# Who reads the second mixer's transposes, and how many copies of the relative bias lie in DRAM

## Chip, cores and metric

The kernel runs on one core of one Trainium2 chip. The metric is the device time of one execution in microseconds (us), the median of several runs. The inputs come from DRAM, the output goes back there.

## What is computed

Two blocks of two layers each on 256 tokens of width 1024. In the first block a layer is a mixer (grouped attention and dilated attention) and a mixture of 16 experts; the second block's layers are a gated linear attention and a differential attention, each followed by a mixture of 16 experts. Two pieces matter here. The first is the start of a layer of the first block: the layer's input is normalised, scaled and shifted by the condition, and multiplied by `w_in`:

```python
for l in range(DEPTH):                       # DEPTH = 2
    mod = cond @ w_ada[l] + b_ada[l]
    sh1, sc1, g1, sh2, sc2, g2 = [m[:, None, :] for m in jnp.split(mod, 6, axis=-1)]
    h = _layer_norm(x) * (1.0 + sc1) + sh1
    mix = _mixer(h, w_in[l], ...)
    x = _layer_norm(DN_ALPHA * x + g1 * mix, ln1_g[l], ln1_b[l])
    h = _layer_norm(x) * (1.0 + sc2) + sh2
    ffn = _moe(h, w_router, router_bias, w_exp_gate[l], w_exp_up[l], w_exp_down[l])
    x = _layer_norm(DN_ALPHA * x + g2 * ffn, ln2_g[l], ln2_b[l])
```

The second is the relative bias of the differential attention, which depends only on the distance of two tokens and the head:

```python
bias = rel_table[rel_bucket(kpos[None, :] - qpos[:, None])].transpose(2, 0, 1)
s = jnp.einsum('bhqd,bhkd->bhqk', qb, kk).astype(jnp.float32) * scale + bias
```

## The kernel before

The 256 tokens are two row tiles of 128. A product with 32-bit weights is made of three: weights and activations are split into a part that is rounded to the matrix engine's format and the rest, `whi` and `wlo`, `hh` and `hl`, and `acc` sums whi·hh, whi·hl and wlo·hh (L427). ScalarE writes `whi` (L346), VectorE and, at the borders between stages, GpSimd write `wlo` (L356). The stages follow each other on the same `x`: mixer 0, moe10, mixer 1, moe11, then the second block with moe20 and moe21; while one stage runs, SyncE loads the weights of those that follow.

**The border.** `block1(l, prev)` is a mixer of the first block. For its second call `prev` is the end of moe10. For each row tile VectorE writes `z` in two halves (L1251), TensorE turns it in two groups of four 128x128 pieces into a PSUM tile `pt` (`transposed`, L321), and `ev` brings each piece to SBUF, scaled by `sc1` and shifted by `sh1`, which are values per partition once `z` is turned. `ev` writes the result twice: ScalarE as `hh` (L1240, rounded by the write), VectorE as `hf` (L1241, unrounded); then VectorE subtracts for `hl` (L1243). `hf` has two buffers. Between the row tiles VectorE finishes `x` of row tile 1 (L297, L302) and GpSimd helps with `wlo`. The products of the first two weight columns start while the second row tile is still underway.

**The relative bias.** `bias_task` runs as a side task of mixer 1. It makes one row of 384 values for each of 8 heads (`fsb`, 8 partitions) and a DMA on ScalarE's queue writes it into DRAM as `fd` (L1542). In the second block `diff` reads it back (L1783), on ScalarE's queue too, so that partition p gets 256 values that begin at 127 − p: row p of the table is the same row shifted by one. The read steps 383 values from partition to partition, so each partition reads a copy of its own. The reads go into buffers that the weights of moe20 leave, while its last `y` products run.

**Order.** Which instruction follows which on an engine is settled when the program is built, by the recorded order of the code and by planners that place side tasks. Loads of weights are issued by SyncE in program order (L193); each waits for its buffer. There are eight semaphores for hardware DMAs, DMAHW0 to DMAHW7, given out in turn over all DMAs of the program, whichever engine issues them; a DMA waits until the one that had its semaphore before, eight DMAs back, has landed.

Of the kernel before, what the change touches and what calls it, by code (L numbers as in the profile page):

```python
# [10 lines left out]
F32 = mybir.dt.float32  # L11
# [3 lines left out]
AF = mybir.ActivationFunctionType  # L15
OP = mybir.AluOpType
# [3 lines left out]
P = 128  # L20
# [96 lines left out]
SM_TICKS = 4  # L117
JOB_GAP = 2
P_BUFS = 4
S_BANKS = 3  # L120
DEC = 4
TAGS = ("moe10", "moe11", "moe20", "moe21")
# [8 lines left out]
def body(ctx: ExitStack, tc: tile.TileContext, A: dict, out: bass.AP, dbg=None):  # L131
    nc = tc.nc
    PE, V, S, G = nc.tensor, nc.vector, nc.scalar, nc.gpsimd
# [9 lines left out]
    dram = ctx.enter_context(tc.tile_pool(name="dr", bufs=1, space=DRAM))  # L143
# [858 lines left out]
    def residual(fl, gp, xh, xl, late, lanes, rows, hold, route, logits, gate=None):  # L1002
# [38 lines left out]
        def scores(tt, k0, m):  # L1041
            if k0 == 0:
                rp[tt] = ps.tile([P, 512], F32, tag="s2", name="rp", bufs=S_BANKS)
            for k in range(k0, k0 + m):
# [117 lines left out]
    def block1(l, prev):  # L1162

        with tc.tile_pool(name="gp", bufs=1, reuse_waits="tile") as gp:
            gates[l, 1] = gp.tile([P, D], F32, name="g2")
            es = gp.tile([P, 2, NE], F32, name="es")
            with ExitStack() as stack:
# [7 lines left out]
                hh = gp.tile([P, KC, T], F32R, tag="hh", name="hh")  # L1175
# [17 lines left out]
                sh1, sc1 = modc[l][:, 0:8], modc[l][:, 8:16]  # L1193
# [41 lines left out]
                def ev(tt, q, pt):  # L1235
                    ts = slice(tt * P, (tt + 1) * P)
                    t = dl.tile([P, 4, P], F32, tag="hf", name="hf", bufs=2)
                    for c in range(4):
                        k = 4 * q + c
                        S.activation(hh[:, k, ts], pt[:, c], AF.Identity, bias=sh1[:, k:k + 1], scale=sc1[:, k:k + 1])  # L1240
                        V.tensor_scalar(t[:, c], pt[:, c], sc1[:, k:k + 1], sh1[:, k:k + 1], op0=OP.mult, op1=OP.add)  # L1241
                    dst = (slice(None), slice(4 * q, 4 * q + 4), ts)
                    V.tensor_tensor(hl[dst], t, hh[dst].bitcast(F32), op=OP.subtract)  # L1243

                if prev is not None:
                    for tt in range(2):
                        if tt == 1:
                            for _ in prev.affine(1):
                                pass
                        for hs in (slice(0, 512), slice(512, 1024)):  # L1250
                            V.tensor_scalar(z[:, tt, hs], X[:, tt, hs], *prev.mr[tt], op0=OP.subtract, op1=OP.mult)  # L1251
                        if tt == 0:
                            prev.second()
                        prev.lows()
                        transposed(ps, "tp", z[:, tt], tt, ev)
                    chain_ends()
# [83 lines left out]
                def global_job(tt, c):  # L1340

                    s2 = [ps.tile([P, 2, 256], F32, tag="s2", name="s2", bufs=S_BANKS) for _ in range(2)]
                    for j in range(2):
# [5 lines left out]
                    for v in range(2):  # L1349
# [3 lines left out]
                        V.scalar_tensor_tensor(nm, nm, -1.0, sc, op0=OP.mult, op1=OP.mult)  # L1353
                        p = d2.tile([P, 2, 256], F32, tag="p", name="p", bufs=P_BUFS)
                        sums = sm.tile([P, 2], F32, tag="sums", name="sums")
# [30 lines left out]
                def dil_job(tt, c):  # L1386
                    pr = []
                    s2 = [ps.tile([P, 512], F32, tag="s2", name="s2d", bufs=S_BANKS) for _ in range(2)]
                    rows_ = [slice(64 * hf, 64 * hf + 64) for hf in range(2)]
# [10 lines left out]
                    for hf in range(2):  # L1400
                        slope = 2.0 ** (-8.0 * (2 * c + hf + 1) / 12)
                        p = d2.tile([P, 384], F32, tag="p", name="pd", bufs=P_BUFS)
                        V.tensor_scalar(p[:, 0:256], nb[:, tt * T:(tt + 1) * T], slope, None, op0=OP.mult)
# [43 lines left out]
                if l + 1 == DEPTH:  # L1447
                    fl.add("ada", bias_task(ps, d2))
# [42 lines left out]
                for u in range(4):  # L1491
                    wh, wl = fl.get()
                    fl.ahead()
                    for m in range(2):
# [4 lines left out]
                        t = dl.tile([P, 2, T], F32, tag="hf", name="mt", bufs=2)  # L1499
# [16 lines left out]


    lam = cst.tile([P, 4], F32, name="lam")
    fd = dram.tile([8, P, 384], F32, name="fd")
    fap = fd[:]  # L1520

    def bias_task(ps, pool):


        oh1 = pool.tile([32, 512], F32, tag="pT", name="ohb", bufs=3)
        S.dma_start(oh1, A["bucket"])
        rt = pool.tile([32, 8], F32, tag="adas", name="rt8")
        S.dma_start(rt, A["rel_table_2"])
        ab = []
        for nm in "qk":  # L1530
            t = pool.tile([P, 128], F32, tag="adab", name="lq")
            for i in range(2):
                src = A[f"b_lam_{nm}{i + 1}_2"][0]
                S.dma_start(t[:, 64 * i:64 * i + 64], bass.AP(tensor=src.tensor, offset=src.offset, ap=[[0, P], [1, 64]]))
            ab.append(t)
        yield LAM_WAIT
        pf = ps.tile([P, 512], F32, tag="tp", name="pf")
        PE.matmul(pf[0:8, :], rt, oh1, start=True, stop=True)
        yield 1
        fsb = pool.tile([8, 384], F32, tag="pT", name="fsb", bufs=3)  # L1540
        V.tensor_copy(fsb, pf[0:8, :384])
        S.dma_start(fd, fsb[:, None, :].to_broadcast([8, P, 384]))  # L1542
        yield 2
        t = pool.tile([P, 128], F32, tag="adas", name="ltm")
        tc.keep_in_program_order(V.tensor_tensor(t, ab[0], ab[1], op=OP.mult))
        V.tensor_reduce(lam[:, 0:2], t.rearrange("p (i e) -> p i e", i=2), axis=AX.X, op=OP.add)
        yield 1
        S.activation(lam[:, 0:2], lam[:, 0:2], AF.Exp)
        V.tensor_tensor(lam[:, 2:3], lam[:, 0:1], lam[:, 1:2], op=OP.subtract)
        V.tensor_scalar(lam[:, 3:4], lam[:, 2:3], LAMBDA_INIT, -1.0, op0=OP.add, op1=OP.mult)  # L1550
# [189 lines left out]
    def diff(prev, gp, room, load_router, logits, rows):  # L1740
        with tc.tile_pool(name="dl", bufs=1, reuse_waits="tile") as dl, tc.tile_pool(name="d", bufs=1, reuse_waits="tile") as d, tc.tile_pool(name="d2", bufs=2, reuse_waits="tile") as d2, \
# [3 lines left out]
            def slot(i, shape, name):  # L1745
                return room[i].tile([P] + shape, F32, tag="w", name=name)

            hh = gp.tile([P, KC, T], F32R, tag="hh", name="hh4")
# [31 lines left out]
            v = [t[:, 0].rearrange("p (t n) -> p t n", t=2) for t in vb]  # L1780
            Tb = [t[:, 1].rearrange("p (h n) -> p h n", h=4) for t in vb]
            for i in range(2):
                S.dma_start(Tb[i], bass.AP(tensor=fap.tensor, offset=fap.offset + 127 + i * 4 * P * 384,  # L1783
                                           ap=[[383, P], [P * 384, 4], [1, 256]]))
            pbuf = slot(7, [4, 2, 256], "pbuf")
            pairs = [(0, 1), (2, 3)]
            gs = row_bcast(d, "gs", A["b_g_sub_2"][0])
# [7 lines left out]
            def job(tt, hp):  # L1795
                nk = (tt + 1) * P
                ws = []
                pair = pairs.pop(0)
                s2 = [ps.tile([P, 512], F32, tag="s2", name="s2f", bufs=S_BANKS) for _ in range(2)]
                for i in range(2):  # L1800
# [80 lines left out]
    def block2(l, prev):  # L1881
        with ExitStack() as es:
            gp = es.enter_context(tc.tile_pool(name="gp", bufs=1, reuse_waits="tile"))
            room = [es.enter_context(tc.tile_pool(name=f"ring{i + 3}", bufs=1, reuse_waits="tile")) for i in range(8)]
            lg, el = gp.tile([P, 2, 4], F32, name="lg"), gp.tile([P, 2, NE], F32, name="el")

            cols = gp.tile([P, 2, KC], F32, name="cols")
            shifts = []

            def load_router():  # L1890
                S.dma_start(cols, A["ln_cols"][:, l])
                route = router(gp, [A["moe_w_group_2"][l], A["moe_w_router_2"][l]],
                               [A["moe_b_group_2"][l], A["moe_b_router_2"][l].rearrange("g j -> (g j)")])
                shifts.append(route[2][:, 1])
                return route, cols

            def logits(tt, t, sd):
                b = shifts[0]
                V.scalar_tensor_tensor(lg[:, tt], t[:, 0:4], sd, b[:, 0:4], op0=OP.mult, op1=OP.add)
                V.scalar_tensor_tensor(el[:, tt], t[:, 4:20], sd, b[:, 4:20], op0=OP.mult, op1=OP.add)  # L1900

            z = (gla if l == 0 else diff)(prev, gp, room, load_router, logits, lambda: rows_of(A["ln_g_2"][l, 0], A["ln_b_2"][l, 0]))
            return moe(z, 2, SLOTS2[l], (lg, el), A["moe_w_gate_2"][l], A["moe_w_up_2"][l], A["moe_w_down_2"][l], None, None,
                       f"moe2{l}", lambda: rows_of(A["ln_g_2"][l, 1], A["ln_b_2"][l, 1], True), False, room=room)
# [49 lines left out]
```

## Time and profile before

| | before |
|---|---|
| median of 3 runs (lowest to highest) | 1602.59 us (1598.65 to 1603.44) |
| profiled execution, and its span | 1602.16 us, 1600.4 us |
| TensorE (PE) busy | 1470.0 us, 92% of the span |
| VectorE (DVE), ScalarE (ACT), GpSimd (POOL) busy | 869.0, 432.8, 129.2 us |
| DMA, mean | 288 GB/s |
| mean granted clock of TensorE | 0.969 of full speed |

Times of rows are in us from the start of the span. A granted clock of 1.00 is the upper of TensorE's two levels (2.4 GHz), 0.50 the lower (1.2 GHz). In a timeline each row gives the start, the time until the end of the last of the instructions put together in it, the engine, the line, the operation and its tiles, their count, and in brackets how long the engine had stood idle before and what released it. Engines with a q are their instruction queues, where a DMA issue counts with the time that the issue itself stood. In a row of waits stand the engine, the line and tile that waited, what it waited for, then the sum, the number of waits and the longest.

### The profile page before, as it was taken

To read this page: it belongs to the slowest core of one execution; us is meant where nothing else is said; L and a number is where in the kernel's file an instruction comes from. 1 tells how busy PE (TensorE), PEld (TensorE's weight loads), DVE (VectorE), ACT (ScalarE), POOL (GpSimd) and SP (SyncE) were. 2 spreads that over 40 slices of the span, in tenths; PEclk is the share of its full clock that TensorE was granted. 3 is DMA by queue.
4 is the path that set the end of the run, shared out by engine and by line. 5 is a ranking of instruction groups with operands and counts; after the bars stand their busy time and mean duration, and the time that the engine had idled before them with its cause. 6 is when DMAs were issued, how large, how long until landed. Compare 5 with 4: busy or idle time off the path is not lost. (4 is left out here: it accounts for less than half of the span.)

```text
span 1600.4 us, 22811 instructions
## 1 busy us (share of the span) xinstructions
PE 1470.0 (92%) x9124; PEld 969.4 (61%) x9124; DVE 869.0 (54%) x1686; ACT 432.8 (27%) x733; POOL 129.2 (8%) x140
## 2 busy tenths in 40 slices
PE   4999987998889999889989999999998999999895
PEld 3879987443478999734448895443337988434331
DVE  3689998343678879823464574231127776212214
ACT  1454331211235434111125331110103652101000
POOL 0200002000121000300011001000003002000001
PEclk9999999999979999889999999999999999999998
DMA  9978799995855769799887487999999966999993
GB/s 301 365 249 273 259 303 324 353 302 198 268 174 173 242 232 337 167 363 359 292 263 214 133 290 267 386 387 353 381 334 288 298 195 244 341 386 387 346 386 124
DMA packets 324371, 461.69 MB, mean 288 GB/s; under 512 B 20077, under 2 KB 178285, under 8 KB 324258
## 3 DMA queue, kind: packets, MB, share of 16 engines
q1 hardware_dynamic: 308720, 446.34, 81.5%
q10 hardware_dynamic: 15538, 13.81, 3.5%
q8 instruction: 76, 1.25, 0.3%
q14 instruction: 37, 0.30, 0.1%
HBM read 456.43 MB, written 3.67 MB: 287 GB/s over the span
## 5 line engine op out<-in xcount | busy, mean ns | idle before, releaser
L786 PE MATMUL gu<-w,xg 128*64 128x512 f32 x1536 | 369.2, 597 | 0.0
L786 PEld LDWEIGHTS gu<-w,xg 128*64 128x64 f32 x1536 | 110.8, 137 | 209.1 <-issue 202.7
L356 DVE TENSOR_TENSOR wlo<-w,whi 128x2048 fp32r<-128x2048 f32 (+2 forms) x92 | 183.3, 1994 | 44.9 <-ACT whi L346 44.2
L850 PE MATMUL y<-w,sa 128*64 128x512 f32 x768 | 195.6, 607 | 4.4 <-DMA w<-in_w_exp_down_dram 4.4
L346 ACT ACTIVATE whi<-w 128x2048 fp32r<-128x2048 f32 (+2 forms) x92 | 157.9, 1726 | 151.4 <-PE acc L427 111.6
L850 PEld LDWEIGHTS y<-w,sa 128*64 128x64 f32 x768 | 55.0, 138 | 106.0 <-issue 97.7
L830 DVE SCALAR_TENSOR_TENSOR sa<-gu,cr,sa 128x256 f32<-128x256 f32 (+1 forms) x32 | 19.7, 615 | 163.6 <-PE gu L786 136.4
L334 PE MATMUL sc<-yy,st 128*128 128x512 f32 x256 | 88.8, 436 | 18.1 <-ACT yy L860 14.3
L522 DVE SCALAR_TENSOR_TENSOR adac<-w,ce,adac 128x512 f32<-128x512 f32 x140 | 104.7, 748 | 1.2
L427 PE MATMUL acc<-hl,whi 128*128 128x256 f32 x608 | 93.3, 286 | 0.0
L427 PE MATMUL acc<-hh,whi 128*128 128x256 f32 x608 | 90.4, 289 | 1.6 <-ACT whi L346 1.6
L892 DVE TENSOR_TENSOR x<-x,sc 128x512 f32<-128x512 f32 x112 | 74.3, 683 | 30.4 <-PE sc L334 30.3
L427 PE MATMUL acc<-hh,wlo 128*128 128x256 f32 x608 | 85.9, 281 | 0.0
L334 PE MATMUL pg<-oh,zh 128*128 128x256 f32 x256 | 73.8, 319 | 13.1 <-DVEq L907 7.3
L334 PEld LDWEIGHTS sc<-yy,st 128*128 128x128 f32 x256 | 42.0, 188 | 70.7 <-ACT yy L860 36.0
L427 PEld LDWEIGHTS acc<-hh,whi 128*128 128x128 f32 x608 | 78.4, 190 | 6.8 <-issue 4.1
L427 PE MATMUL acc<-whi,hh 128*128 128x256 f32 x416 | 70.9, 303 | 12.2 <-ACT hh L1240 8.9
L427 PEld LDWEIGHTS acc<-hl,whi 128*128 128x128 f32 x608 | 79.6, 189 | 3.7 <-issue 3.2
L427 PEld LDWEIGHTS acc<-hh,wlo 128*128 128x128 f32 x608 | 77.3, 188 | 1.0 <-issue 0.8
L334 PEld LDWEIGHTS pg<-oh,zh 128*128 128x128 f32 x256 | 55.4, 218 | 27.8 <-issue 15.0
L334 PE MATMUL pg<-oh,zl 128*128 128x256 f32 x256 | 71.2, 308 | 0.9 <-issue 0.9
L860 ACT ACTIVATE yy<-y 128x512 fp32r<-128x512 f32 x32 | 19.1, 597 | 192.2 <-PE y L850 192.2
(376 smaller groups left out, 2107.8 us busy)
## 6 DMA issues: line engine op xcount, KB each, us to landing
w<-in_moe_w_gate_dram SPq DMA_DIRECT2D x64, 1024.0 KB, 12.1
w<-in_moe_w_up_dram SPq DMA_DIRECT2D x64, 1024.0 KB, 13.8
w<-in_moe_w_down_dram SPq DMA_DIRECT2D x128, 512.0 KB, 11.6
w<-in_w_ada_dram SPq DMA_DIRECT2D x47, 1024.0 KB, 7.2
w<-in_w_in_dram SPq DMA_DIRECT2D x40, 1024.0 KB, 5.6
w<-in_w_exp_gate_dram SPq DMA_DIRECT2D x64, 512.0 KB, 9.5
w<-in_w_exp_up_dram SPq DMA_DIRECT2D x64, 512.0 KB, 8.8
w<-in_w_exp_down_dram SPq DMA_DIRECT2D x64, 512.0 KB, 8.9
```

The costliest lines, as they stand in the source:

```text
L334: PE.matmul(dst, l, r, start=(i == 0), stop=(i == n - 1), skip_group_check=True)
L346: S.activation(hi[:, k0:k0 + n], w, AF.Copy)
L356: eng.tensor_tensor(lo[:, k0 + x:k0 + y], w[:, x:y], hi[:, k0 + x:k0 + y].bitcast(F32), op=OP.subtract)
L427: PE.matmul(dst, l, r, start=(start and i == 0), stop=(i == n - 1), skip_group_check=True)
L522: V.scalar_tensor_tensor(acc, ws[k // 4][:, k % 4], ce[:, k:k + 1], acc, op0=OP.mult, op1=OP.add)
L786: PE.matmul(gu[64 * j:64 * j + 64, :], xg[:, 4 * kh + k, (2 * pr + j) * CAP:(2 * pr + j + 1) * CAP], ws[j][:, k, :], start=(kh == 0 and k ...
L830: V.scalar_tensor_tensor(sg, u, cr, sg, op0=OP.mult, op1=OP.mult)
L850: PE.matmul(y[64 * j:64 * j + 64, :], aT[:, f, 64 * j:64 * j + 64], w[:, j, k, :], start=(f == 0), stop=(f == NF - 1), tile_position=(0, 6 ...
L860: S.activation(yh[:, hs], src, AF.Copy)
L892: V.tensor_tensor(X[:, tt, hs], X[:, tt, hs], sc, op=OP.add)
```

## The change

`ev` changes: ScalarE writes the scaled and shifted pieces unrounded to `hf`, four for each half of a row tile; VectorE then writes `hh` from `hf` in one copy with rounding, and subtracts as before. VectorE doesn't read `pt` any more. `fd` holds 32 copies of each row instead of 128, and each of the two reads becomes four, of 32 partitions each, which read the same 32 copies from starting points that lie 32 values apart.

```diff
+FD = 32
@@ ev, in block1
                     for c in range(4):
                         k = 4 * q + c
-                        S.activation(hh[:, k, ts], pt[:, c], AF.Identity, bias=sh1[:, k:k + 1], scale=sc1[:, k:k + 1])
-                        V.tensor_scalar(t[:, c], pt[:, c], sc1[:, k:k + 1], sh1[:, k:k + 1], op0=OP.mult, op1=OP.add)
+                        S.activation(t[:, c], pt[:, c], AF.Identity, bias=sh1[:, k:k + 1], scale=sc1[:, k:k + 1])
                     dst = (slice(None), slice(4 * q, 4 * q + 4), ts)
+                    V.tensor_copy(hh[dst], t)
                     V.tensor_tensor(hl[dst], t, hh[dst].bitcast(F32), op=OP.subtract)
@@ the bias in DRAM
-    fd = dram.tile([8, P, 384], F32, name="fd")
+    fd = dram.tile([8, FD, 384], F32, name="fd")
@@ bias_task
-        S.dma_start(fd, fsb[:, None, :].to_broadcast([8, P, 384]))
+        S.dma_start(fd, fsb[:, None, :].to_broadcast([8, FD, 384]))
@@ diff
             for i in range(2):
-                S.dma_start(Tb[i], bass.AP(tensor=fap.tensor, offset=fap.offset + 127 + i * 4 * P * 384,
-                                           ap=[[383, P], [P * 384, 4], [1, 256]]))
+                for p0 in range(0, P, FD):
+                    S.dma_start(Tb[i][p0:p0 + FD], bass.AP(tensor=fap.tensor, offset=fap.offset + 127 - p0 + i * 4 * FD * 384,
+                                                           ap=[[383, FD], [FD * 384, 4], [1, 256]]))
```

The new lines shift the numbers: a line of before stands one lower after the constant, and one more lower behind the loop of reads.

On VectorE, at the border, before (`s_` are statistics, `modc` holds `sc1` and `sh1`):

```order
L356 TENSOR_TENSOR wlo<-w,whi 128x512
L1241 TENSOR_SCALAR hf<-pt,modc 128x128 x4
L1243 TENSOR_TENSOR hl<-hf,hh 128x4x128
L1241 TENSOR_SCALAR hf<-pt,modc 128x128 x4
L1243 TENSOR_TENSOR hl<-hf,hh 128x4x128
L297 SCALAR_TENSOR_TENSOR x<-x,mv,rows 128x1024
```

and after:

```order
L357 TENSOR_TENSOR wlo<-w,whi 128x512
L1243 CAST hh<-hf 128x4x128
L1244 TENSOR_TENSOR hl<-hf,hh 128x4x128
L1243 CAST hh<-hf 128x4x128
L1244 TENSOR_TENSOR hl<-hf,hh 128x4x128
L298 SCALAR_TENSOR_TENSOR x<-x,mv,rows 128x1024
```

In the place of four evictions stands one CAST; row tile 1 has the same pattern behind its own `wlo` and `z`.

On TensorE, at the start of row tile 1 of the border, with the semaphores that each waits for (DVE for VectorE, Activation for ScalarE, Pool for GpSimd), before:

```order
L321 MATMUL pt<-consts,z 128x128 [waits DVE_49]
L321 MATMUL pt<-consts,z 128x128 x3
L427 MATMUL acc<-whi,hh 128x256 [waits Activation_49]
L427 MATMUL acc<-wlo,hh 128x256 [waits DVE_49]
L427 MATMUL acc<-wlo,hh 128x256 x3
L427 MATMUL acc<-wlo,hh 128x256 [waits Pool_49]
L427 MATMUL acc<-wlo,hh 128x256
L427 MATMUL acc<-wlo,hh 128x256 [waits Pool_49]
L427 MATMUL acc<-wlo,hh 128x256
L427 MATMUL acc<-whi,hh 128x256 [waits Activation_49] x7
L427 MATMUL acc<-whi,hl 128x256 [waits DVE_49]
L427 MATMUL acc<-whi,hl 128x256 x3
```

and after:

```order
L322 MATMUL pt<-consts,z 128x128 [waits DVE_49,Activation_49]
L322 MATMUL pt<-consts,z 128x128 x3
L428 MATMUL acc<-wlo,hh 128x256 [waits DVE_49]
L428 MATMUL acc<-wlo,hh 128x256 x3
L428 MATMUL acc<-wlo,hh 128x256 [waits Pool_49]
L428 MATMUL acc<-wlo,hh 128x256
L428 MATMUL acc<-wlo,hh 128x256 [waits Pool_49]
L428 MATMUL acc<-wlo,hh 128x256
L428 MATMUL acc<-whi,hh 128x256 [waits DVE_49]
L428 MATMUL acc<-whi,hh 128x256 x3
L428 MATMUL acc<-whi,hh 128x256 [waits DVE_49]
L428 MATMUL acc<-whi,hh 128x256 x3
```

The `whi,hh` products waited for ScalarE one by one, the first of them ahead of `wlo,hh`; now all eight stand behind `wlo,hh` and wait for VectorE twice. The products `whi,hl` follow in both. On ScalarE the eviction `qtok` of the first weight columns (L1450), which stood behind ten of the 16 evictions of `ev`, stands behind all of them.

On SyncE, at the end of moe20's loads, before:

```order
L193 DMA w<-in_moe_w_up_dram 128x4x512 [waits DMAHW0_49,PE_49]
L193 DMA w<-in_moe_w_down_dram 128x2x512 [waits DMAHW2_49,PE_49]
L193 DMA w<-in_moe_w_down_dram 128x2x512 [waits DMAHW3_49]
L193 DMA w<-in_moe_w_down_dram 128x2x512 [waits DMAHW4_49,PE_49]
L193 DMA w<-in_moe_w_down_dram 128x2x512 [waits DMAHW6_49]
L193 DMA w<-in_moe_w_down_dram 128x2x512 [waits DMAHW7_49,PE_49]
L193 DMA w<-in_moe_w_down_dram 128x2x512 [waits DMAHW0_49]
L193 DMA w<-in_moe_w_down_dram 128x2x512 [waits DMAHW1_49,PE_49]
```

and after:

```order
L194 DMA w<-in_moe_w_up_dram 128x4x512 [waits DMAHW0_49,PE_49]
L194 DMA w<-in_moe_w_down_dram 128x2x512 [waits DMAHW3_49,PE_49]
L194 DMA w<-in_moe_w_down_dram 128x2x512 [waits DMAHW5_49]
L194 DMA w<-in_moe_w_down_dram 128x2x512 [waits DMAHW7_49,PE_49]
L194 DMA w<-in_moe_w_down_dram 128x2x512 [waits DMAHW1_49]
```

The semaphore DMAHW1 belongs to the first read of `fd` in both; the load that waits for it is the seventh w_down before and the fourth after. Behind it, after, the seventh, eighth, tenth and thirteenth load wait for the fourth, fifth, sixth and eighth read.

On ScalarE's queue, at the same place, before:

```order
L794 ACTIVATE sa<-gu 128x512 [waits PE_49]
L1783 DMA vb<-fd 128x4x256 [waits DMAHW6_49,DMAHW1_49,PE_49]
L1783 DMA vb<-fd 128x4x256 [waits DMAHW7_49,DMAHW5_49,PE_49]
L860 ACTIVATE yy<-y 128x512 [waits DVE_49,PE_49]
L860 ACTIVATE yy<-y 128x512 [waits PE_49]
```

and after:

```order
L795 ACTIVATE sa<-gu 128x512 [waits PE_49]
L1785 DMA vb<-fd 32x4x256 [waits DMAHW6_49,DMAHW1_49,PE_49]
L1785 DMA vb<-fd 32x4x256 [waits DMAHW2_49]
L1785 DMA vb<-fd 32x4x256 [waits DMAHW4_49]
L1785 DMA vb<-fd 32x4x256
L1785 DMA vb<-fd 32x4x256 [waits DMAHW7_49,DMAHW0_49,PE_49]
L1785 DMA vb<-fd 32x4x256 [waits DMAHW2_49]
L1785 DMA vb<-fd 32x4x256 [waits DMAHW4_49]
L861 ACTIVATE yy<-y 128x512 [waits DVE_49,PE_49]
L1785 DMA vb<-fd 32x4x256 [waits DMAHW7_49]
L861 ACTIVATE yy<-y 128x512 [waits PE_49]
```

Seven reads stand ahead of the first `yy`, the eighth behind it.

## Rows read from the trace of the kernel before

**Rows 1.** The page, part 1: busy time, share and instructions.

```profile
PE 1470.0 (92%) x9124; PEld 969.4 (61%) x9124; DVE 869.0 (54%) x1686; ACT 432.8 (27%) x733; POOL 129.2 (8%) x140
```

**Rows 2.** Waits between 432 and 462 us: sum, times, longest.

```profile
ACT hh L1240 <- DVE hf L1241: 10.2, 11, 2.0
PE acc L427 <- ACT hh L1240: 8.9, 11, 1.9
```

**Rows 3.** Stretches: length, busy time of each engine, clock, DMA share, GB/s.

```profile
432.00:462.00 30.00, 19.18 (x77) 15.14 (x77) 21.16 (x37) 7.58 (x17) 10.67 (x13) 0.70 0.40 114
464.00:520.00 56.00, 52.79 (x429) 48.11 (x429) 46.33 (x76) 28.78 (x49) 9.82 (x6) 1.00 0.65 212
600.00:655.00 55.00, 51.83 (x403) 49.06 (x402) 51.23 (x98) 17.52 (x23) 1.53 (x1) 0.97 0.98 312
```

**Rows 4.** Timeline of the border, row tile 0, 431 to 443 us.

```profile
432.12 0.46 ACT L1240 ACTIVATE hh<-pt,modc 128x128 fp32r<-128x128 f32 x1 [5.22 <-PE pt L321]
...
434.45 3.71 POOL L356 TENSOR_TENSOR wlo<-w,whi 128x512 fp32r<-128x512 f32 x3
...
435.37 0.46 ACT L1240 ACTIVATE hh<-pt,modc 128x128 fp32r<-128x128 f32 x1 [0.48 <-DVE hf L1241]
435.86 0.41 DVE L1241 TENSOR_SCALAR hf<-pt,modc 128x128 f32<-128x128 f32 x1 [0.53 <-ACT hh L1240]
...
436.31 0.81 ACT L1240 ACTIVATE hh<-pt,modc 128x128 fp32r<-128x128 f32 x2 [0.48 <-DVE hf L1241]
...
437.25 1.46 DVE L1243 TENSOR_TENSOR hl<-hf,hh 128x512 fp32r<-128x512 f32 x1
...
441.88 0.69 DVE L1243 TENSOR_TENSOR hl<-hf,hh 128x512 fp32r<-128x512 f32 x1
```

**Rows 5.** Timelines of VectorE, ScalarE and TensorE, row tile 1, 443 to 462 us.

```profile
447.82 2.89 DVE L1251 TENSOR_SCALAR z<-x,mv,rs 128x512 f32<-128x512 f32 x2 [0.66 <-POOL rs L203]
450.64 1.34 DVE L356 TENSOR_TENSOR wlo<-w,whi 128x1024 fp32r<-128x1024 f32 x1
...
450.06 0.46 ACT L1240 ACTIVATE hh<-pt,modc 128x128 fp32r<-128x128 f32 x1 [8.66 <-PE pt L321]
...
460.32 2.02 PE L427 MATMUL acc<-whi,hl 128*128 128x256 f32 x8
```

**Rows 6.** Groups by form, 432 to 462 us: count, busy us, mean ns, idle before.

```profile
L520 DVE TENSOR_SCALAR adac<-w,ce 128x512 f32<-128x512 f32 x1 | 0.5, 480 | 0.0
```

**Rows 7.** Queue of the write, 647 to 678 us; timelines of the issues, 640 to 710.

```profile
q10 hardware_dynamic: 1016, 1.56, 40.7%
...
645.63 1.27 ACTq L1542 DMA_DIRECT2D fd<-fsb  x1
...
653.09 4.99 SPq L193 DMA_DIRECT2D w<-in_w_exp_up_dram  x1
...
663.28 11.31 SPq L193 DMA_DIRECT2D w<-in_w_exp_up_dram  x1
```

**Rows 8.** Timeline of TensorE, 690 to 712 us, and the stretch 700 to 710.

```profile
701.33 1.94 PE L850 MATMUL y<-w,sa 128*64 128x512 f32 x2 [3.00 <-DMA w<-in_w_exp_down_dram]
704.67 6.37 PE L850 MATMUL y<-w,sa 128*64 128x512 f32 x14 [1.40 <-DMA w<-in_w_exp_down_dram]
...
700.00:710.00 10.00, 7.27 (x15) 1.92 (x16) 0.92 (x2) 0.63 (x1) 0.00 (x0) 0.50 1.05 381
```

**Rows 9.** moe20's end: SyncE's waits, landings, TensorE's timeline, 1155 to 1207 us.

```profile
SPq L193 <- DMA vb<-fd: 13.4, 2, 10.3
...
w<-in_moe_w_down_dram SPq DMA_DIRECT2D x16, 512.0 KB, 8.4
...
DMA to landing us min/median/max: 3.6/4.5/5.4
...
1185.40 1.94 PE L850 MATMUL y<-w,sa 128*64 128x512 f32 x8
...
1189.64 3.65 PE L850 MATMUL y<-w,sa 128*64 128x512 f32 x16
```

## The prediction

> **What bounds the kernel now.** I read the page's busy shares first: TensorE works for 1470.0 of the 1600.4 us span [rows 1], so time can be won where TensorE stands or runs at its lower clock, and nowhere else. The waits of TensorE then give two places that the diff touches. The first is the second mixer's border (432 to 462 us): TensorE is busy 19.18 of 30 us and has 0.70 of its clock, DMA is at 0.40 [rows 3]; it waits for ScalarE's `hh` 11 times, 8.9 us, and ScalarE for VectorE's `hf` 11 times, 10.2 us [rows 2]. The timeline shows why: both engines read the same transposed tile in turn, never together. ScalarE 0.46 us, VectorE 0.41 us, ScalarE again at 0.94 us from its last start; two ScalarE pieces without VectorE between them take 0.81 us [rows 4]. The second place is the first expert of moe11 (698 to 711 us): `y` waits twice for its weights, and then works at clock 0.50 [rows 8]. The weights are late because the DMA that writes `fd` is in the way from 645.63 on [rows 7].
>
> **Part A, the border.** Removed are 16 VectorE evictions, four for each half of a row tile; added is one CAST of 128x512 from SBUF to SBUF for each half. ScalarE keeps 16 evictions, now one behind the other at 0.405 us (0.81 for two).
>
> No row shows this CAST. The nearest is VectorE's 128x512 TENSOR_SCALAR from SBUF, 480 ns [rows 6]; the subtraction behind it takes 0.69 us alone and 1.46 us while GpSimd splits weights [rows 4]. So CAST and subtraction take 1.2 us unhindered; hindered like that subtraction (2.1 times) 2.5 us; hindered like `z`, which took 2.89 us beside GpSimd [rows 5], 3.4 us (2.89 for two is 1.45 each, three times 0.48; three times 0.69 is 2.0).
>
> Row tile 0: ScalarE starts at 432.12; eight evictions end at 435.4. VectorE stands in a weight split until 434.1 and has the first four by then. Two pairs of CAST and subtraction end at 436.5, 439.1 or 441.0; before, the second subtraction ended at 442.57 (441.88 + 0.69) [rows 4]. Gain 6.1, 3.5 or 1.6 us. I take the middle one, since GpSimd's three splits lie at 434.45 to 438.16, on these very instructions. From the second subtraction to `z` of row tile 1 (447.82) VectorE works through its own list without a wait worth naming, so `z` comes earlier by as much.
>
> Row tile 1, on the old times: ScalarE's first eviction at 450.06, VectorE's weight split until 451.98 (450.64 + 1.34) [rows 5]. Then CAST, subtraction, CAST, and four matmuls `whi,hh` of 0.25 us (2.02 for eight [rows 5]) until `whi,hl` can start: 451.98 + 0.5 + 0.7 + 0.5 + 1.0 = 454.7; with 1.5 us of GpSimd's hindrance 456.2; at three times 457.9. Before it was 460.32 [rows 5]. The eight `wlo,hh` ahead of them take 2 us and fit into that time. Gain 5.6, 4.1 or 2.4 us.
>
> Sum of A: 3.5 + 4.1 = 7.6 us, bounds 4.0 and 11.7. I take 7.5. It should stay: from 464 to 655 TensorE is busy 52.79 of 56 us at full clock and, at the end, 51.83 of 55 [rows 3], and no instruction there waits for a transfer, so the whole list moves forward. VectorE is at 51.23 of 55 us at the end, near its bound, but its list moves forward as well.
>
> TensorE's new waits: `whi,hh` now waits for VectorE, once for four matmuls, instead of for ScalarE at each. Behind the CAST on VectorE stand its own subtraction and the `x` chain, which waited there before too. ScalarE's `qtok` now stands behind all 16 evictions instead of the tenth; `qtok` frees an accumulator that TensorE has no use for until the first `whi,hl`. I cost both at nothing; if that cover is gone, it is one eviction row, 0.5 us.
>
> **Part B1, the copies written.** The write's queue shows 1016 packets in 31 us, 40.7% of the time of 16 engines [rows 7], and 1024 rows of 1.5 KB are to be written: 33 a microsecond. With 256 rows it lasts 7.8 us and ends near 654 instead of 678. In those 31 us SyncE's issues stand for 4.99 and 11.31 us at a time [rows 7]; so the weights of moe11 start some 20 us earlier. What `y` then finds: it could start at 698.33 (701.33 − 3.00) and take 3.65 us for 16 matmuls, as in moe20 [rows 9], ending at 702.0; it ended at 711.04 (704.67 + 6.37) [rows 8]. That is 9.1 us: 4.4 us of waits (3.00 + 1.40) and 4.7 us of half clock. The clock was 0.50 in 700 to 710 [rows 8], right behind the 3.00 us wait, and full before it, so I take both as gone. Bounds: 4.4 (the waits alone) and 9.1; a loss is excluded, since fewer bytes go through the same queue. I take 9.1. With A the gathers before moe11 come 7.5 us earlier, but a lead of 20 us on the weights covers that.
>
> **Part B2, the copies read.** Two reads become eight, on ScalarE's queue, where six of them fit into its pause ahead of the first `yy`; each costs 0.38 us of issue there. What matters is SyncE. Every DMA waits for the DMA eight places before it in the program. The seventh of moe20's last 16 w_down loads waited for the first read: 10.3 us [rows 9], and TensorE never noticed. With six more DMAs woven in, the *fourth* load waits for it. Three loads of 512 KB move from before the pause to after it, while `y` still starts at 1185.40 and 1189.64 [rows 9]. The fourth is issued near 1182. Landing in 3.6 us, like the first read [rows 9], it serves 1185.4 with 0.2 us lacking, and what follows lands at some 1.5 us each against four matmuls of 0.23 us and `sc` between. Landing in 8.4 us, the loads' median there [rows 9], it is 5 us late. TensorE had no slack to give back, so below nothing is excluded. Bounds 0 and 5; I take 1.0, near the lower, because the transfers have drained when it is issued. Later loads wait for the fourth, fifth, sixth and eighth read, which are out by then.
>
> Against splitting speaks the Trainium skill, "DMA: Bandwidth & Descriptors", section "Rules for kernel authors": one transfer over 128 partitions instead of several over parts of them, and by its "Anatomy of one DMA" each pays about 2.0 us fixed. If the four reads of a half paid that in turn, they would take 8 us, an estimate from that page; the fifth read's waiter would be late and this term about 3 us, the sum 1588.6. Reads in flight together would not pay in turn, and no run here shows it yet.
>
> **Sum**, from the profiled execution of 1602.16 us, 0.4 us under the median of 1602.59: 1602.2 − 7.5 − 9.1 + 1.0 = **1586.6 us**.
>
> **The rivals.**
> *GpSimd holds VectorE up.* CAST and subtraction move between SBUF tiles while GpSimd splits weights. If every one is held up like `z` [rows 5], A is 4.0: 1602.2 − 4.0 − 9.1 + 1.0 = 1590.1. For it: the CAST lands on GpSimd's 3.71 us [rows 4]. Against: the subtraction suffered less there than `z`. The Trainium skill, "SBUF — State Buffer", section "SBUF: two separate sides", has GpSimd and VectorE's copies between SBUF tiles lock each other out for whole instructions, and would have this rival; the 1.46 against 0.69 us [rows 4] agrees with it. Chance 0.20.
> *The border is given back:* VectorE, 51.23 of 55 us busy before 655, or the mixer's transfers set the pace, and only the copies pay: 1602.2 − 9.1 + 1.0 = 1594.1. Against: no such wait between 464 and 655. Chance 0.10.
> *The write doesn't do what the diff says:* it holds its engines as long with a quarter of the rows, or something else holds SyncE, and only the border pays: 1602.2 − 7.5 + 1.0 = 1595.7. Against: packets leave evenly, at 33 a microsecond. Chance 0.10.
> *Slower: moe20's `y` starves.* Each of the four groups of 16 matmuls between 1181 and 1205 waits as `y` did at 701 (3.00 us), and the clock falls to half, 3.65 us more for each group: 4 × 6.65 = 26.6 us, 1602.2 − 16.6 + 26.6 = 1612.2. It decides from 4.2 us a group (16.6 / 4). For it: the re-ordered waits. Against: loads land at 1.5 us each once they flow. Chance 0.05.
>
> **How the numbers follow.** Forecast 0.50, the rivals 0.20, 0.10, 0.10 and 0.05, and neither part paying (about 1600) 0.05. A measurement here can tell 0.3%, 4.8 us, from no change: faster means below 1597.8. All but the last two cases are below; of the border-only case a part is not (with A at 4.0 it ends at 1599.2). So faster 0.87, same 0.08, slower 0.05. The range goes from both gains at their upper bounds (1602.2 − 11.7 − 9.1 = 1581.4) to the border-only case: 1581 to 1596.
>
> **What would show it.** Border: ScalarE's `hf` in a row at about 0.4 us, VectorE's CAST at 0.5 to 1.5 us, `whi,hl` of row tile 1 some 7.5 us earlier. Write: the queue's packets gone within 8 us, no 11 us stand of SyncE, no wait at `y` in moe11, its clock 1.00. Read: SyncE's fourth w_down load released by the first read; TensorE waiting for w_down around 1185 minus 16 by up to some microseconds. I am wrong if the mixer's end (655) moves by less than 4 us, if `y` in moe11 still waits, or if moe20's end shows half clock.

## The result, and the profile after

The changed kernel takes 1583.69 us, median of 4 runs (1581.42 to 1588.59), against 1603.01 us before (1598.65 to 1605.08): a ratio of 0.9887, 95% interval 0.9855 to 0.9919. Run again beside two experiments it took 1583.5 us against 1602.38, a ratio of 0.9883 (0.9866 to 0.99). The profiled execution took 1584.98 us, its span is 1582.5 us. The forecast was 1586.6 us.

Page of the changed kernel, part 1:

```profile
PE 1460.8 (92%) x9124; PEld 964.2 (61%) x9124; DVE 864.9 (55%) x1674; ACT 431.7 (27%) x733; POOL 130.6 (8%) x140
```

TensorE does the same 9124 matmuls, in 9.2 us less of busy time than before [rows 1]; as these are the same products, that part of the gain is clock. To see where the other part comes from I read the start of the same five instructions on ScalarE in both timelines: the border's first eviction (432.12 before), `lam` behind the write of `fd` (646.96), the first eviction after moe11 (831.91), the last `sa` of moe20 (1175.20) and the first `whi` behind moe20 (1205.74).

| stretch | before | after | gain |
|---|---|---|---|
| first eviction of the border to `lam` | 214.84 | 204.97 | 9.9 |
| `lam` to the end of moe11 | 184.95 | 173.41 | 11.5 |
| to the last `sa` of moe20 | 343.29 | 343.39 | −0.1 |
| last `sa` to the first `whi` behind moe20 | 30.54 | 33.87 | −3.3 |
| to the end of the span | 394.66 | 394.74 | −0.1 |

In these two profiles all of the 17.9 us between the spans lies in the three places that the diff touches.

**The border.** Timeline of the changed kernel:

```profile
432.12 2.90 ACT L1241 ACTIVATE hf<-pt,modc 128x128 f32<-128x128 f32 x8 [5.21 <-PE pt L322]
...
433.98 0.42 DVE L1243 CAST hh<-hf 128x512 fp32r<-128x512 f32 x1
434.44 0.69 DVE L1244 TENSOR_TENSOR hl<-hf,hh 128x512 fp32r<-128x512 f32 x1
434.45 4.91 POOL L357 TENSOR_TENSOR wlo<-w,whi 128x512 fp32r<-128x512 f32 x3
...
435.05 1.49 DVE L1243 CAST hh<-hf 128x512 fp32r<-128x512 f32 x1
436.57 1.64 DVE L1244 TENSOR_TENSOR hl<-hf,hh 128x512 fp32r<-128x512 f32 x1
...
438.14 2.30 DVE L298 SCALAR_TENSOR_TENSOR x<-x,mv,rows 128x1024 f32<-128x1024 f32 x1
...
444.50 2.88 DVE L1252 TENSOR_SCALAR z<-x,mv,rs 128x512 f32<-128x512 f32 x2 [0.66 <-POOL rs L204]
...
452.28 1.66 PE L428 MATMUL acc<-whi,hl 128*128 128x256 f32 x8
```

ScalarE's eight evictions of row tile 0 stand in one row without a wait, 2.90 us, where it took turns before [rows 4]. The second subtraction ends at 438.21 instead of 442.57, `z` starts at 444.50 instead of 447.82, and row tile 1's `whi,hl` at 452.28 instead of 460.32 [rows 5]. The stretch that answers to the first of [rows 3]:

```profile
432.00:462.00 30.00, 22.16 (x150) 20.95 (x150) 27.25 (x33) 10.82 (x20) 12.76 (x13) 0.83 0.56 177
```

150 matmul records instead of 77 in the same 30 us, and a clock of 0.83 instead of 0.70.

**moe11.** The queue of the write in the changed kernel, 636 to 646 us:

```profile
q10 hardware_dynamic: 264, 0.39, 27.3%
```

The first issues of SyncE behind it:

```profile
641.48 2.99 SPq L194 DMA_DIRECT2D w<-in_w_exp_up_dram  x1
644.52 0.50 SPq L194 DMA_DIRECT2D w<-in_w_exp_gate_dram  x1
```

The first `y` on TensorE's timeline:

```profile
685.87 3.65 PE L851 MATMUL y<-w,sa 128*64 128x512 f32 x16
```

The longest stand of a load is 2.99 us, not 11.31 [rows 7], and `y` is one row of 16 matmuls in 3.65 us that waits for nothing, where it was two rows at half clock, with 4.4 us of waits ahead of them [rows 8].

**The end of moe20.** Waits of SyncE (1135 to 1185 us, then 1161 to 1178 alone), the landings of the reads, and the waits of TensorE (1150 to 1195):

```profile
SPq L194 <- DMA vb<-fd: 19.7, 5, 11.5
...
SPq L194 <- DMA vb<-fd: 8.3, 4, 4.6
...
DMA to landing us min/median/max: 2.4/4.4/8.0
...
PE y L851 <- DMA w<-in_moe_w_down_dram: 2.0, 3, 0.8
```

TensorE's timeline there:

```profile
1168.97 1.93 PE L851 MATMUL y<-w,sa 128*64 128x512 f32 x6 [0.57 <-DMA w<-in_moe_w_down_dram]
1171.46 1.07 PE L851 MATMUL y<-w,sa 128*64 128x512 f32 x2 [0.56 <-DMA w<-in_moe_w_down_dram]
1173.36 2.49 PE L851 MATMUL y<-w,sa 128*64 128x512 f32 x8 [0.83 <-DMA w<-in_moe_w_down_dram]
```

SyncE waits five times for a read, not twice [rows 9], and `y`, which waited for no load before, waits three times. Two of its groups are stretched beyond their waits as well: 2.49 us for eight matmuls against 1.94 for the eight in [rows 9].

### The profile page after: what moved, and what is told of

Its sections match the earlier page's. It is cut to its first block, busy times and chain, and to the rows that moved or that the text cites. A ratio compares the mean times of both kernels' runs of the same rounds, so it can differ in the third digit from the quotient of the medians.

```text
span 1582.5 us, 22807 instructions
## 1 busy us (share of the span) xinstructions
PE 1460.8 (92%) x9124; PEld 964.2 (61%) x9124; DVE 864.9 (55%) x1674; ACT 431.7 (27%) x733; POOL 130.6 (8%) x140
## 3 DMA queue, kind: packets, MB, share of 16 engines
HBM read 456.43 MB, written 2.49 MB: 290 GB/s over the span
## 5 line engine op out<-in xcount | busy, mean ns | idle before, releaser
L428 PE MATMUL acc<-whi,hh 128*128 128x256 f32 x416 | 65.7, 295 | 6.4 <-DVE hh L1243 3.3
L823 DVE TENSOR_SCALAR st<-pst 128x256 fp32r<-128x256 f32 x24 | 10.2, 423 | 110.8 <-ACT pst L822 110.8
## 6 DMA issues: line engine op xcount, KB each, us to landing
w<-in_moe_w_down_dram SPq DMA_DIRECT2D x128, 512.0 KB, 11.3
```

Source lines behind the costliest of these rows:

```text
L428: PE.matmul(dst, l, r, start=(start and i == 0), stop=(i == n - 1), skip_group_check=True)
L823: V.tensor_scalar(st, pst[:, :T], 0.0, None, op0=OP.is_gt)
```

## The experiments

The table gives for each kernel the ratio to the kernel before on the same chip, and the gain in the stretches of the table above, each against the one profile of before. Kernels with a border like the changed one show 9.5 to 11.8 us in the first column, those whose write no longer holds the weights 8.9 to 11.7 in the second. The column "moe11 to `sa`" holds nothing that any of these kernels touches; it moves between −3.4 and 1.7, and that is what one profile can't tell. (The last stretch, which isn't in the table, moves between −2.7 and 0.8.) The first column is steadier: e2 and e3, whose border is the old one, show 1.2 and 0.4, and the changed kernel itself 9.9 and, as e10, 11.1; its first profile has a clock of 0.57 in 484 to 488 us, where e10 has 1.00.

| kernel | median us | ratio (95%) | border | moe11 | moe11 to `sa` | moe20's end |
|---|---|---|---|---|---|---|
| e1 border alone | 1591.44 | 0.9940 (0.9923 to 0.9957) | 11.2 | 1.1 | 1.3 | 0.0 |
| e2 copies alone | 1592.93 | 0.9947 (0.9931 to 0.9963) | 1.2 | 11.5 | 1.7 | −3.7 |
| e3 split reads alone | 1605.34 | 1.0012 (0.9996 to 1.0028) | 0.4 | −0.4 | −0.2 | −3.5 |
| e4 border, wide write | 1583.00 | 0.9880 (0.9860 to 0.9899) | 11.5 | 11.2 | −3.4 | 0.0 |
| e5 64 copies | 1587.13 | 0.9916 (0.9884 to 0.9947) | 11.1 | 10.3 | 1.7 | −2.2 |
| e6 ScalarE rounds | 1584.68 | 0.9891 (0.9865 to 0.9917) | 9.5 | 10.6 | −1.7 | −3.8 |
| e7 grouped evictions | 1591.65 | 0.9934 (0.9915 to 0.9954) | 10.6 | −0.3 | 0.2 | 0.0 |
| e8 e4 with e6 | 1582.20 | 0.9886 (0.9855 to 0.9917) | 10.1 | 9.6 | 1.5 | 0.0 |
| e9 no GpSimd at the border | 1582.08 | 0.9870 (0.9849 to 0.9892) | 13.6 | 8.9 | 1.2 | −3.3 |
| e10 the changed kernel again | 1583.50 | 0.9883 (0.9866 to 0.9900) | 11.1 | 11.7 | 1.3 | −2.9 |
| e11 e4 again | 1579.66 | 0.9863 (0.9840 to 0.9885) | 11.8 | 9.7 | 1.4 | 0.0 |
| e12 e4 with e7's border | 1582.72 | 0.9873 (0.9852 to 0.9894) | 10.5 | 10.9 | −0.1 | 0.0 |

**e1 to e3: the parts one by one.** e1 has the new `ev` and the old copies and reads, e2 the new copies and reads and the old `ev`. e3 writes 128 copies as before and only splits the reads:

```diff
-                S.dma_start(Tb[i], bass.AP(tensor=fap.tensor, offset=fap.offset + 127 + i * 4 * P * 384,
-                                           ap=[[383, P], [P * 384, 4], [1, 256]]))
+                for p0 in range(0, P, 32):
+                    S.dma_start(Tb[i][p0:p0 + 32], bass.AP(tensor=fap.tensor, offset=fap.offset + 127 + 383 * p0 + i * 4 * P * 384,
+                                                           ap=[[383, 32], [P * 384, 4], [1, 256]]))
```

> The border's change alone, 128 copies and two reads as before. Theory (the three parts add up: border 9.9 us by the ends of ScalarE's evictions in the two traces, copies 11.5, reads -3.4): 9.9 us faster, 1592 to 1593; w_in products of row tile 1 start near 452.3 instead of 460.3; y of moe11 still waits some 4 us for its weights and works at clock 0.5. Rival (2.4 of the 11.5 us ahead of moe11's y come from the border's shift of the clock, not from the copies): 12 us faster, near 1590.

> 32 copies and eight reads, the border as before. Theory: the write lasts 8 us, y of moe11 waits for nothing, 11.5 - 3.4 = 8 us faster, near 1594; first y of moe20's last columns waits about 2 us for w_down. Rival (the 2.4 us ahead of y come from the border): 5.7 us faster, near 1596.5.

> 128 copies written as before, but read in eight parts of 32 partitions; the border as before. Theory (the reads' order on the eight DMA semaphores costs 3.4 us at moe20's end): 3 to 4 us slower, near 1606; y waits for w_down about 2 us in three pieces, SyncE's fourth w_down load stands for the first read. Rival (the waits at moe20's end come from having only 32 copies, read four times over): no difference, 1602.

The parts add up: 10.9 us (1602.38 − 1591.44) and 9.4 us alone, 20.4 together, against 19.3 and 18.9 for the changed kernel. e3 is 3.0 us slower in its median; its interval reaches down to no difference, but in the stretch itself the loss is 3.5 us, as with 32 copies, so it is the splitting that costs and not that the copies are read four times. Waits of TensorE in e3, at moe20's end (1170 to 1220 us) and at moe11 (665 to 715 us):

```profile
PE y L850 <- DMA w<-in_moe_w_down_dram: 2.2, 4, 0.9
...
PE y L850 <- DMA w<-in_w_exp_down_dram: 7.0, 2, 5.6
```

The second row leads to where 2.4 of the 11.5 us at moe11 come from. Before, TensorE ran at half clock behind a wait of 2.75 us that ended at 671.93, where the routing of moe11 starts (`pos`) and the gathers (`pg`) follow. Stretches of before:

```profile
672.00:676.00 4.00, 2.75 (x17) 2.66 (x17) 2.39 (x12) 0.16 (x1) 1.23 (x2) 0.58 0.59 93
676.00:680.00 4.00, 4.00 (x14) 2.17 (x14) 1.09 (x2) 0.96 (x2) 0.00 (x0) 0.57 0.89 244
```

In e3, with the same write, the clock is full there:

```profile
672.00:676.00 4.00, 3.78 (x23) 2.84 (x24) 2.34 (x7) 1.13 (x2) 1.23 (x2) 1.00 0.74 148
676.00:680.00 4.00, 4.00 (x25) 2.24 (x26) 1.09 (x2) 2.41 (x3) 0.00 (x0) 1.00 0.90 254
```

e3's TensorE is there 2.5 us earlier, counted from `lam`, and stands at `y` 2.6 us longer, 7.0 instead of 4.4 us. As long as the write held the weights, the loads set the end of this `y`, and what TensorE won or lost ahead of it was invisible. Without the write TensorE sets it. So the rival that gave these 2.4 us to the border's shift falls: e2 has them without the border, and e1, with the border, has 1.1 and a `y` that waits 5.6 us.

The half clock isn't absent in e3; it lies earlier. Between 660 and 668 us, under `warm` matmuls that only fill the time until `pos` (L997), e3 has a clock of 0.61, and the changed kernel has 0.61 in 652 to 660, under the router's products and its own `warm`. There it costs little: `pos` needs VectorE's `r_m` too and comes 24.8 to 26.5 us behind `lam` in every profile. In e9, whose write is short too, the half clock lies behind `pos` as before. Wait ahead of `pos` and stretch of e9:

```profile
PE pos L726 <- DVE r_m L559: 2.7, 1, 2.7
...
660.00:668.00 8.00, 6.99 (x27) 5.16 (x28) 3.10 (x12) 1.13 (x2) 1.23 (x2) 0.57 1.06 372
```

e9 gains 8.9 us at moe11. In the ten profiles whose write no longer holds the weights the gain goes with this place: 10.6 to 11.7 us where TensorE doesn't wait ahead of `pos`, 9.6 to 10.3 where it waits 1.1 us (e5, e8, e11), 8.9 where it waits 2.7 (e9). e4 and e11 are the same kernel and gain 11.2 and 9.7, so the place doesn't belong to the kernel. The same stretch in e4, then in e11:

```profile
660.00:668.00 8.00, 7.17 (x47) 5.77 (x46) 5.12 (x23) 1.47 (x3) 2.54 (x5) 1.00 1.07 362
...
660.00:668.00 8.00, 5.67 (x28) 4.24 (x27) 5.00 (x23) 1.13 (x2) 2.45 (x5) 0.79 1.07 363
```

With the half clock where it lay before, the short write is worth 8.9 us; up to 2.8 more depend on where it falls.

**e4 and e11: is it the rows or the engines of the write?** The row of values is made twice for each head, on 16 partitions, and the write starts from these; 128 copies and two reads as before:

```diff
-        rt = pool.tile([32, 8], F32, tag="adas", name="rt8")
-        S.dma_start(rt, A["rel_table_2"])
+        rt = pool.tile([32, 8, 2], F32, tag="adas", name="rt8")
+        rsrc = A["rel_table_2"]
+        S.dma_start(rt[:, :, :, None], bass.AP(tensor=rsrc.tensor, offset=rsrc.offset, ap=[[8, 32], [1, 8], [0, 2], [1, 1]]))
...
-        PE.matmul(pf[0:8, :], rt, oh1, start=True, stop=True)
+        PE.matmul(pf[0:16, :], rt.rearrange("p h r -> p (h r)"), oh1, start=True, stop=True)
...
-        S.dma_start(fd, fsb[:, None, :].to_broadcast([8, P, 384]))
+        S.dma_start(fd.rearrange("h (r c) n -> (h r) c n", r=2), fsb[:, None, :].to_broadcast([16, P // 2, 384]))
```

> The border's change, 128 copies and two reads as before, but the row of values is made on 16 partitions, two for each head, so that the write starts from 16 partitions instead of 8. Theory (what held moe11's weights up is that the write keeps some 7 of 16 engines for 31 us): the write is shorter, 13 to 20 us over all 16 engines; y of moe11 waits for nothing, no wait for w_down at moe20's end; 9.9 + 11.5 = 21 us faster than before, near 1581. Rival (it is the number of 1.5 KB rows, not how they lie on the engines): the weights are held as long, y waits, near 1592.

> The kernel of e4_wide (border changed, row of values on 16 partitions, 128 copies, two reads). Theory (its trace lost 4.8 us to a stretch at half clock at the start of the gated linear attention, which no part of it explains, and saved the 3.4 us of the split reads): over more runs 2 to 4 us under the changed kernel, near 1581. Rival (the stretch at half clock belongs to this kernel): level with the changed kernel.

The measure beside e11, the changed kernel itself:

> The changed kernel as it is, as the measure for the two kernels beside it: 1583 to 1585.

Queue and landing of the write in e4, 636 to 653 us:

```profile
q10 hardware_dynamic: 1040, 1.57, 70.7%
...
fd<-fsb ACTq DMA_DIRECT2D x1, 1536.0 KB, 17.8
```

The same 1024 rows of 1.5 KB take 70.7% of 16 engines for 17 us instead of 40.7% for 31 us [rows 7]: 192 and 202 us of engine time, about equal work on 1.7 times as many busy engines. That is enough: moe11's `y` waits for no load, and moe20's end costs nothing, since there are two reads again. The Trainium skill, "DMA: Bandwidth & Descriptors", section "Rules for kernel authors", says that an outermost dimension of fewer than 16 confines a transfer to at most that many engines; 8 partitions at 40.7%, which is 6.5 of 16 engines, and 16 partitions at 70.7%, 11.3 of them, agree.

e4's trace loses 3.4 us between moe11 and `sa`, to a clock of 0.50 in 836 to 844 at the start of the gated linear attention. e11, the same kernel, doesn't have it (1.4), so it doesn't belong to the kernel. The nine times of this kernel, e4 and e11 together, have a median of 1581.96 us, the eight of the changed kernel, e10 included, 1583.50. Side by side on one chip it is 1579.66 against 1583.50; the intervals, 0.9840 to 0.9885 and 0.9866 to 0.9900, overlap. The stretch says that 3 us are saved, the totals don't yet tell it.

**e5: half as many reads.**

```diff
-FD = 32
+FD = 64
```

> The changed kernel with 64 copies instead of 32, so four reads of 64 partitions instead of eight. By the order of the semaphores the fifth w_down load of moe20's end stands for the first read, not the fourth. Theory (the reads' place among the loads costs, by how many loads must wait): about 1.5 to 2.5 us of the 3.4 come back, moe11's y still waits for nothing since the write ends well before; near 1582. Rival (the cost is eight small transfers as such, or 32 partitions at a time): with half as many, half the cost, the same 1.7 us, but w_down waits in y are as many as in the changed kernel. Rival 2: a write twice as long (16 us) brings moe11's wait back, 1587 or more.

Waits of TensorE at moe20's end in e5:

```profile
PE y L851 <- DMA w<-in_moe_w_down_dram: 1.6, 2, 1.4
```

The fifth load now stands for the first read. The stretch costs 2.2 us instead of 3.3, `y` waits twice instead of three times, and moe11's `y` waits for nothing with twice as many rows to write. 2.2 lies outside the 2.9 to 3.8 us of the kernels with eight reads. The direction is the theory's, the size smaller than expected (1.1 instead of 1.5 to 2.5 us come back); a price for each small read, the rival, isn't excluded by it. The total, 1587.13, is above the changed kernel's: two of its four times are near 1590, and its trace loses another 1.4 us behind this stretch at a clock of 0.50 (1198 to 1206 us). So e5 doesn't show that 64 copies are better.

**e6 and e8: ScalarE makes the rounded copy too.**

```diff
-                    V.tensor_copy(hh[dst], t)
+                    S.activation(hh[dst], t, AF.Copy)
```

> The changed kernel, but ScalarE makes the rounded copy hh from hf too (128x512, SBUF to SBUF), VectorE only subtracts. Theory (beside GpSimd's splits VectorE's CAST and subtraction are stretched, 1.49 and 1.64 us in row tile 0, so an operation less on VectorE there is time gained): w_in's second row tile starts 1 to 2 us earlier, near 1582. Rival (what ends the border is TensorE's own work at half clock, not VectorE): within 0.5 us of the changed kernel.

> The border with ScalarE making hf and hh (as e6_castact), the write from 16 partitions with 128 copies and two reads (as e4_wide). Theory: the parts add up, 1 to 2 us under e4_wide's 1583.0, near 1581. Rival: as e4_wide.

Nothing is won: 9.5 and 10.1 us at the border, totals level with the kernels they build on. ScalarE's copy takes 0.63 us, and in row tile 1 the second one stands behind `qtok` on ScalarE, which waits for TensorE, so the second subtraction came at 450.31, 0.9 us later than in the changed kernel when both are counted from the border's first eviction (19.5 against 18.6 us).

**e7 and e12: no copy at all, only another order.** `ev` of before, with ScalarE's four pieces first and VectorE's four behind them:

```diff
                     for c in range(4):
                         k = 4 * q + c
                         S.activation(hh[:, k, ts], pt[:, c], AF.Identity, bias=sh1[:, k:k + 1], scale=sc1[:, k:k + 1])
+                    for c in range(4):
+                        k = 4 * q + c
                         V.tensor_scalar(t[:, c], pt[:, c], sc1[:, k:k + 1], sh1[:, k:k + 1], op0=OP.mult, op1=OP.add)
```

> The kernel before, only the order of ev's evictions changed: ScalarE's four pieces first, then VectorE's four, both still from PSUM; copies and reads as before. Theory A (what the border lost is the turn-taking piece by piece on one PSUM tile): most of the 10 us come back without any copy, 1593 to 1596. Theory B (it is VectorE's 16 evictions themselves, 0.41 us each against one CAST of 0.42): at most 4 us, 1598 to 1601.

> As e11_wide, but with the grouped evictions of e7_grouped instead of the CAST (ScalarE's four, then VectorE's four, from PSUM). Theory (what the border gains is the end of the turn-taking): level with e11_wide within 2 us, near 1581. Rival (the CAST adds a gain of its own that e7_grouped hid): 3 us or more over e11_wide.

Timeline of e7, row tile 0:

```profile
431.82 2.91 ACT L1240 ACTIVATE hh<-pt,modc 128x128 fp32r<-128x128 f32 x8 [5.21 <-PE pt L321]
...
433.69 1.36 DVE L1243 TENSOR_SCALAR hf<-pt,modc 128x128 f32<-128x128 f32 x4
435.08 0.88 DVE L1245 TENSOR_TENSOR hl<-hf,hh 128x512 fp32r<-128x512 f32 x1
435.89 1.35 DVE L1243 TENSOR_SCALAR hf<-pt,modc 128x128 f32<-128x128 f32 x4
```

This is the clearest answer of the study. With the same 32 evictions, both engines reading PSUM, the border gives 10.6 us (1591.65 us in all), as much as e1's 1591.44. ScalarE reads one tile `pt` while VectorE reads the other; four evictions of VectorE take 1.36 us in a row instead of 3.2 (three turns of 0.94 and a last eviction of 0.41 [rows 4]). What the border had lost is the turn-taking, piece by piece, on one tile. That VectorE stops reading PSUM, and that its 16 evictions become four CASTs, adds nothing measurable: theory B falls. e12 puts the same border under the wide write and is level with it within the intervals.

**e9: GpSimd kept out of the border.** `lows` gets a share, which this border alone sets to 8 eighths, so that VectorE makes all of `wlo`:

```diff
-                        prev.lows()
+                        prev.lows(8)
```

> The changed kernel, but at this border VectorE makes all of wlo and GpSimd none (the three and two splits of 128x512 go to VectorE). Theory (the CAST took 1.49 us and the subtractions up to 1.64 because GpSimd's splits ran): both CASTs of row tile 0 take about 0.42 us, the subtractions 0.69, z of row tile 1 near 1.0 us for two instead of 2.88; VectorE's first split takes 2.3 us instead of 0.69, its second 2.3 instead of 1.34. The border ends within 1 us of the changed kernel. Rival (the CAST is slow by itself when TensorE or ScalarE reads the same tiles): the second CAST stays near 1.5 us.

Timeline of e9:

```profile
436.70 0.42 DVE L1243 CAST hh<-hf 128x512 fp32r<-128x512 f32 x1
437.15 0.69 DVE L1244 TENSOR_TENSOR hl<-hf,hh 128x512 fp32r<-128x512 f32 x1
...
437.76 0.42 DVE L1243 CAST hh<-hf 128x512 fp32r<-128x512 f32 x1
438.22 0.69 DVE L1244 TENSOR_TENSOR hl<-hf,hh 128x512 fp32r<-128x512 f32 x1
...
444.16 1.01 DVE L1252 TENSOR_SCALAR z<-x,mv,rs 128x512 f32<-128x512 f32 x2 [0.66 <-POOL rs L204]
```

All of VectorE's stretched operations are back at their own length: 0.42 against 1.49 us, 0.69 against 1.64, 1.01 for two `z` against 2.88. VectorE pays with longer splits, and the border still has the largest gain of all, 13.6 us. The Trainium skill, "SBUF — State Buffer", section "SBUF: two separate sides", lets GpSimd and VectorE's copies between SBUF tiles exclude each other for a whole instruction. The traces agree as far as they go: without GpSimd's splits the stretching is gone, and beside VectorE's CAST the splits were stretched too, 4.91 us for three; that one engine stood for whole instructions of the other no row shows. The total, 1582.08 us in two runs, can't be told from the changed kernel's. This border under the wide write was not run.

## Why the prediction was right

The range (1581 to 1596) holds the time, and all three terms had the right sign and place. Their sizes were off, in ways that partly cancelled: that the sum comes within 3 us of the time is in part luck.

**Part A, 7.6 us worked out, 9.9 measured (9.5 to 11.8 over the kernels with this border or e7's).** Row tile 0: the second subtraction was put at 439.1 and came at 438.21, since the first CAST and subtraction ended before GpSimd's splits hurt them; but VectorE's `x` behind it took 2.30 instead of 1.28 us for the same reason, so `z` came 3.3 us earlier, near the 3.5 used. Row tile 1: `whi,hl` 8.0 us earlier against 7.6. What was missing is a term behind it: before, TensorE has a clock of 0.50 from 458 to 464, and in the changed kernel, with the denser work, 1.00. The cause was named too narrowly. I costed the CAST against the evictions; e7 shows that only the order mattered. The given-back rival falls by the third to fifth row of the first table: nothing is lost until `lam`, or later.

**GpSimd as a rival.** It was there: the second CAST of row tile 0 took 1.49 us. It hit one pair and `x` and `z`, not every operation, and e9 puts the price of it at some 2 to 4 us of this border (13.6 against 9.9 and 11.1).

**Part B1, 9.1 us worked out, 11.5 measured, with 9.1 as the upper bound.** The bound was wrong. It took `y`'s start from TensorE's own progress in the profile before, and overlooked that this progress contained a stretch at half clock that cost nothing while the loads set `y`'s end. e3 shows that it was hidden. On the clock of before the 9.1 is right: e9, with the half clock in the same place, has 8.9. The 2.4 us above it are luck as far as the runs show, since the changed kernel's half clock fell ahead of `pos`, where it costs little. The write itself did as worked out: 264 packets of the queue instead of 1016, no long stand of SyncE.

**Part B2, 1.0 us worked out, 3.3 measured.** The failed step is one sentence: that the later loads wait for reads "which are out by then". The fourth load was nearly in time. But the fifth read, issued at 1160.73, was not there for SyncE until 1166.57, and SyncE stood 4.6 us for it, with nine of the 16 loads still to be issued; the sixth and the eighth held it again. `vb` landings are 2.4 to 8.0 us, since the reads run beside 512 KB loads. TensorE met this as three short waits at full clock, so the slower rival, which needed 3 us waits and half clock in four groups, never came near. By the sentence on the Trainium skill in the prediction this term was 3 us and the sum 1588.6, with the fifth read's waiter late, as it turned out. That the number fits is luck, for its reason, four reads that pay 2.0 us each in turn, doesn't hold: the first two, issued 0.4 us apart, landed 2.4 and 2.7 us after their issue, so they were under way together. (The section of the Trainium skill named there gives its 2.0 us for DMAs that GpSimd issues; these reads go out on ScalarE's queue.) The fifth read was issued 2.0 us behind the fourth, and SyncE got past it only 5.8 us later, beside the loads. By rows alone I had taken the wrong end.

**The sum.** −7.5 − 9.1 + 1.0 = −15.6 was forecast, −9.9 − 11.5 + 3.3 = −18.1 came, and the medians moved by 19.3 us.

## What to carry to other kernels

Two engines that evict the same PSUM tile should not take it in turns piece by piece: let one finish its pieces while the other works on the neighbouring tile. In this kernel that order alone was worth 10 us in a stretch of 30.

A DMA is priced by what it holds up, not by its bytes: 1.5 MB from 8 partitions took 31 us and made TensorE wait for weights, from 16 partitions they took 17 and it didn't. And splitting a DMA shifts the semaphores of all DMAs behind it; follow who now waits for whom before calling the pieces free.

## What the runs showed of the hardware

- A wait that is set by transfers hides what TensorE's clock does ahead of it: e3 came 2.5 us earlier to moe11's `y` and stood 2.6 us longer, 7.0 us. With the loads out of the way a stretch of half clock there costs more behind `pos` than ahead of it: 8.9 us gained in e9, 11.7 in e10.
- The same kernel has its stretches of half clock in different places from profile to profile: e4 lost 3.4 us in the gated linear attention, e11 won 1.4 there.
- Beside GpSimd's splits, the CAST of 128x512 took 1.49 us instead of 0.42, the subtraction 1.64 instead of 0.69, and GpSimd's three splits 4.91 us instead of 3.71 [rows 4].
- A read of 128 KB beside loads took up to 8.0 us to land; the 512 KB read of before took 3.6 to 5.4 [rows 9].
